# ConvGLU stage: block sums taken from the high and low parts of the stream, and one load list, five blocks ahead, for the down projection

## The chip, the core and the metric

The kernel runs on one core of one Trainium2 chip. Its engines are TensorE (PE; PEld is its weight load), VectorE (DVE), ScalarE (ACT), GpSimd (POOL) and SyncE (SP). SP issues most DMAs; POOL and ACT have queues of their own. The metric is the device time of one execution in microseconds (us); the time of a kernel is the median over runs. All arithmetic is in float32.

## What is computed

One layer of a hybrid backbone over 1024 latent tokens of width 1024 (and 256 context tokens): a mixer, an output projection with a gated residual, then a gated feed-forward network with a 3x3 depthwise convolution on its gate branch, and a last norm. The change lies in the feed-forward part, which is, with x the stream after the mixer (D_FF is 2816):

```python
h = modulate(rmsnorm(x, norm2_g), shift2, scale2)
g = h @ ffn_w_gate                       # 1024 x 2816
u = h @ ffn_w_up
g = dwconv2d_grid(g, conv_w, conv_b)     # 3x3 over a 16 x 64 grid
x = x + gate2 * ((silu(g) * u) @ ffn_w_down)
out = rmsnorm(x, final_norm_g)
```

## The kernel before

**High and low parts.** A float32 product is made of three TensorE products: each operand r is cast to a rounded h (`nc.scalar.copy`, on ACT), and l = r - h is taken on DVE (`tt`) or POOL (`ptt`); then hh, hl and lh are added in PSUM. `split` (L1444) does this for a weight block of 128x512 and gives tiles `wh` and `wl`. `raw` (L1434) loads a block into one of 20 buffers named `rw` by a DMA of the SP queue.

**Norm of the feed-forward's input.** `norm2(t)`, L1313 to L1333, runs for each of 8 tiles of 128 tokens: sum of squares on ACT (into the tile `u`, two buffers), `ss` to a power on POOL, scale on DVE, shift on POOL or DVE, 8 transposes on PE into two PSUM banks `bk`, then for each bank the cast into `mxh` (ACT, L1327) and the low part into `mxl` (DVE). It also copies each bank back over `u` (ACT, L1331) and stores that to DRAM (`ub_d`, SP, L1332), and it stores the stream for the last residual (`x1_d`, SP, L1333; the trace and the lists call it `x_d`).

**First gate and up blocks.** The first two gate columns are plain products of `mxh`, `mxl` (`fmm`, L1302). Their results `im` go through `conv`: for each of two images one ACT instruction and eight taps, `fac<-im,v,fac` at L107 on DVE. The first two up products follow (`up0`), also at L1302.

**Eleven pairs by seven products.** The other 10 pairs of gate columns and 10 of up columns (with `NP` = 11 pairs in all) are made by a seven-product scheme (`group7`, L1519, `bmm` at L1464): seven products of 12 matmuls in place of eight. It needs sums of weight blocks (`rw<-rw,rw`, POOL) and four sums of stream blocks T1 to T4. The four blocks B11, B12, B21, B22 of the transposed stream come back from `ub_d` for these, 16 loads of 256 KB; DVE subtracts, ACT casts into `tq`, and DVE or POOL takes the low parts. T4 overwrites a block that the first products still read, so its cast (L1629) comes after `up0`.

**Sums for the down projection.** While pair j runs, `asums(j)` stores seven blocks of silu(g)*u and their sums to `sa_d`, and `wsums(j)` loads four blocks of `ffn_w_down` and stores their four sums to `sw_d`. `wsums(10)` comes after the last product of the last group.

**Down projection.** Seven products P1, P4, P2, P6, P7, P5, P3 of 11 blocks each, 12 matmuls to a block, at L1692 (`mul`, `product`). A block needs two loads of 256 KB, one from `sa_d` and one from `ffn_w_down` or `sw_d`, both split with the low part on DVE. Each block's loads are written where it is used. P3 has 8 blocks that are split early and stay on the chip (`ahead`, L1757). The stream for the residual, `x1r`, 8 loads of 512 KB (L1713), and the row `gfrow` (L1728) are loaded by SP, written after P1.

**What sets the order.** A scheduler decides at build time in which order each engine runs its instructions, from the order in which they are written and from the buffers that they wait for. Each engine and each DMA queue then takes its list strictly in order.

Of the kernel before, what the change touches and what calls it, by code (L numbers as in the profile page):

```python
# [13 lines left out]
ALU = mybir.AluOpType  # L14
# [59 lines left out]
def hybrid_layer(ctx: ExitStack, tc: tile.TileContext, x, c, cx, c_ctx, w_ada, b_ada, norm1_g, w_in,  # L74
# [69 lines left out]
    ub_d = [T(drp, [NLC, P, 512], f"ub_d{i}") for i in range(2)]  # L144
# [1160 lines left out]
    with pool("op") as op:  # L1305
# [9 lines left out]
        def norm2(t):  # L1315
# [4 lines left out]
            pbs = []  # L1320
            for i in range(2):
# [93 lines left out]
    ASUM = "DDPP"  # L1415
    NR = NTL // GW
# [102 lines left out]
    def group7(w, fa, fb):  # L1519
        st = {}  # L1520

        def prep(n):
            if n == 0:
                st["a11"], st["a21"], st["a22"], st["a12"] = (
                    raw(wcols(w, i, f)) for (i, f) in ((0, fa), (0, fb), (1, fb), (1, fa)))
# [65 lines left out]

    im0 = first_im
# [3 lines left out]
    upw0 = [[raw(wcols(w_up, i, f)) for i in range(2)] for f in FORD[:2]]  # L1596


    late_t4 = []
    for u in range(4):  # L1600
        b11, b12, b21, b22 = (raw(ub_d[i][u + 4 * h]) for i in range(2) for h in range(2))
        t1, t2 = raw(), raw()
        tt(t1, b12, b11, ALU.subtract)
        tt(t2, b22, t1, ALU.subtract)
        tt(b12, b22, b12, ALU.subtract)
        tt(b21, t2, b21, ALU.subtract)
        for n_, t, on_pool in (("T2", t2, u % 2), ("T3", b12, 1), ("T1", t1, u % 2)):
            h, l = (m[:, u, :, :].rearrange("p k t -> p (k t)") for m in BLK[n_])
            nc.scalar.copy(h, t)
            (ptt if on_pool else tt)(l, t, h.bitcast(F32), ALU.subtract)  # L1610
        late_t4.append(b21)
        if u == 1:
            ups_ = [split(r, False) for r in upw0[0]]

    up0 = []
    for b in range(2):
        if b:
            ups_ = [split(r) for r in upw0[1]]
# [8 lines left out]
    for u in range(4):  # L1627
        h, l = (m[:, u, :, :].rearrange("p k t -> p (k t)") for m in BLK["T4"])
        nc.scalar.copy(h, late_t4[u])  # L1629
        ptt(l, late_t4[u], h.bitcast(F32), ALU.subtract)  # L1630
# [9 lines left out]
    preps, ready = {}, {}  # L1640
    AHEAD = 4

    def prepare(i):
        k, j, n = prods[i]
        if n == 0:
            preps[k, j] = group7(w_gate if k == "g" else w_up, FORD[2 * j], FORD[2 * j + 1])
        ready[i] = preps[k, j](n)
# [4 lines left out]
    for i, (k, j, n) in enumerate(prods):  # L1652
# [25 lines left out]
    STA = dict(P1=0, P2=1, P4=2, P3=3, P5=4, P6=5, P7=6)  # L1678
    MOV = dict(P5=0, P6=1, P7=2, P4=3)
    WD = dict(P1=(0, 0), P2=(1, 0), P3=(1, 1))  # L1680

    def sources(p, j):
        if p in MOV:
            return sa_d[STA[p]][j], sw_d[MOV[p]][j]
        k, d = WD[p]
        return sa_d[STA[p]][j], w_down[(j + NP * k) * P:(j + NP * k + 1) * P, 512 * d:512 * d + 512]
# [7 lines left out]
    def product(p, acc, js, first, last, between=None):  # L1694
        for j in js:
            ops = [split(raw(src), False) for src in sources(p, j)]
            for t in range(4):
                mul(acc[t], t, ops, first and j == js[0], last and j == js[-1])
            if between is not None:
                between(j)  # L1700
# [11 lines left out]
    for t in range(NLC):  # L1712
        nc.sync.dma_start(x1[t], x1_d[t])  # L1713
# [14 lines left out]
    nc.sync.dma_start(gf, final_norm_g.partition_broadcast(P))  # L1728
# [24 lines left out]

    HEAD = NP - NLC
    rest = []

    def ahead(*at):  # L1757
        def f(j):
            if j not in at:
                return  # L1760
# [82 lines left out]
```

## Time and profile before

| | |
|---|---|
| runs of the kernel before, us | 1575.12, 1579.88, 1582.5; median 1579.88 |
| the profiled execution, us | 1586.62, of which its span 1584.9 |
| granted TensorE clock over the span | 0.954 |
| busy: PE, DVE, POOL, ACT | 1414.9 (89%), 1159.8 (73%), 793.6 (50%), 745.9 (47%) |
| mixer | to about 790 us |
| output projection, `norm2`, first gate and up blocks | 790 to 909.7 us |
| pairs by seven products | 921.96 to 1336.5 us |
| down projection | 1359.43 to about 1577 us |

The times of a row of the trace are start and length in us. Matmuls are pipelined, so a row of 0.39 us stands for one that takes 0.23 us of PE in a row of them. A bracket at the end of a row gives how long the engine had been idle and which instruction or DMA ended that.

### The profile page before, as it was taken

What the parts mean: (1) busy time and instruction counts of PE and PEld (TensorE: products, weight loads), DVE (VectorE), ACT (ScalarE), POOL (GpSimd) and SP (SyncE); (2) the same over time, 40 slices, a digit from 0 to 9 for tenths busy, and PEclk for the clock granted to TensorE, in tenths of its full rate; (3) what the DMA queues carried; (4) which work ended last, traced back from release to release, by engine and by line L of the source; (5) the groups of instructions that cost most, each with busy time, mean ns of one, the idle gap of its engine ahead of it and who ended that gap; (6) DMA issues with size and microseconds to landing.
All of it is one profiled execution on the core that took longest, in us unless ns stands there. A gap on an engine that the chain in (4) does not pass through costs nothing. (4 is left out here: it accounts for less than half of the span.)

```text
span 1584.9 us, 24483 instructions
## 1 busy us (share of the span) xinstructions
PE 1414.9 (89%) x8104; PEld 1170.3 (74%) x8104; DVE 1159.8 (73%) x1861; ACT 745.9 (47%) x1671; POOL 793.6 (50%) x778
## 2 busy tenths in 40 slices
PE   6899888899998899998985958999999997699997
PEld 2477777787888789997764746877777775588786
DVE  5877698887545757457975679989988997357686
ACT  6566655636666746444254243333333331355453
POOL 3554499782216874201381287678888885000001
PEclk8999999999999999999996979999999999799999
DMA  7344777654669774436953243444444443966732
GB/s 265 122 144 136 233 223 211 162 147 115 181 193 305 224 236 149 152 96 229 336 191 139 96 144 107 146 159 154 152 147 160 153 153 132 399 216 212 216 115 106
DMA packets 273917, 283.54 MB, mean 179 GB/s; under 512 B 52448, under 2 KB 195421, under 8 KB 273791
## 3 DMA queue, kind: packets, MB, share of 16 engines
q1 hardware_dynamic: 266991, 261.41, 52.0%
q0 software_dynamic: 5456, 17.82, 3.1%
q10 hardware_dynamic: 1344, 2.75, 0.5%
q8 instruction: 64, 1.05, 0.3%
q14 instruction: 62, 0.51, 0.1%
HBM read 200.26 MB, written 81.65 MB: 178 GB/s over the span
## 5 line engine op out<-in xcount | busy, mean ns | idle before, releaser
L1444 ACT CAST wh<-rw 128x512 fp32r<-128x512 f32 x282 | 164.7, 620 | 311.2 <-POOL rw L98 107.8
L98 POOL TENSOR_TENSOR wl<-rw,wh 128x512 fp32r<-128x512 f32 x142 | 197.5, 1408 | 88.6 <-ACT wh L1444 85.2
L107 DVE SCALAR_TENSOR_TENSOR fac<-im,v,fac 128x945 f32<-128x945 f32 (+2 forms) x176 | 210.2, 1211 | 33.2 <-ACT fac L92 31.8
L1464 PE MATMUL pb<-mxh,wh 128*128 128x512 f32 x320 | 128.0, 400 | 29.2 <-ACT wh L1444 12.3
L1464 PE MATMUL pb<-tq,wh 128*128 128x512 f32 x480 | 147.3, 391 | 4.2 <-ACT wh L1444 4.2
L95 DVE TENSOR_TENSOR wl<-rw,wh 128x512 fp32r<-128x512 f32 x140 | 92.6, 701 | 61.5 <-ACT wh L1444 61.5
L456 PE MATMUL bk<-hh,wh 128*128 128x512 f32 x320 | 130.0, 407 | 1.6 <-ACT up L506 0.9
L456 PE MATMUL bk<-hh,wl 128*128 128x512 f32 x320 | 130.2, 407 | 0.0
L456 PE MATMUL bk<-hl,wh 128*128 128x512 f32 x320 | 129.0, 403 | 0.0
L1464 PE MATMUL pb<-mxl,wh 128*128 128x512 f32 x320 | 126.8, 396 | 0.3 <-POOL mxl L98 0.3
L1464 PE MATMUL pb<-mxh,wl 128*128 128x512 f32 x320 | 126.5, 395 | 0.0
L1747 POOL TENSOR_TENSOR ss<-ss,mhalf 128x1 f32<-128x1 f32 x8 | 7.3, 918 | 231.8 <-DVE ss L95 231.7
L98 POOL TENSOR_TENSOR rw<-rw,rw 128x512 f32<-128x512 f32 x80 | 110.1, 1387 | 10.5 <-DMA rw<-in_ffn_w_up_dram 5.5
L1464 PEld LDWEIGHTS pb<-tq,wh 128*128 128x128 f32 x480 | 90.4, 189 | 24.1 <-ACT wh L1444 5.4
L1464 PEld LDWEIGHTS pb<-mxh,wh 128*128 128x128 f32 x320 | 61.3, 192 | 46.0 <-issue 16.4
L1464 PE MATMUL pb<-tq,wl 128*128 128x512 f32 x240 | 92.0, 390 | 2.0 <-POOL wl L98 2.0
L95 DVE TENSOR_TENSOR rw<-rw,rw 128x512 f32<-128x512 f32 x60 | 68.7, 1166 | 8.2 <-DMA sa_d<-rw 5.6
L456 PEld LDWEIGHTS bk<-hh,wh 128*128 128x128 f32 x320 | 62.0, 194 | 14.4 <-ACT up L506 1.1
L456 PEld LDWEIGHTS bk<-hh,wl 128*128 128x128 f32 x320 | 61.9, 193 | 13.2 <-issue 0.9
L1692 PE MATMUL im<-wh,wh 128*128 128x512 f32 x144 | 51.0, 395 | 23.0 <-ACT wh L1444 23.0
L1464 PEld LDWEIGHTS pb<-mxl,wh 128*128 128x128 f32 x320 | 61.5, 192 | 13.2 <-POOL mxl L98 0.7
L1464 PEld LDWEIGHTS pb<-mxh,wl 128*128 128x128 f32 x320 | 61.4, 192 | 13.1
(410 smaller groups left out, 4148.3 us busy)
## 6 DMA issues: line engine op xcount, KB each, us to landing
rw<-in_ffn_w_down_dram SPq DMA_DIRECT2D x77, 256.0 KB
rw<-sa_d SPq DMA_DIRECT2D x77, 256.0 KB
kv<-kv_d SPq DMA_DIRECT2D x80, 192.0 KB
yq<-yq_d SPq DMA_DIRECT2D x64, 192.0 KB
awa<-in_w_ada_dram SPq DMA_DIRECT2D x24, 512.0 KB
rw<-in_ffn_w_up_dram SPq DMA_DIRECT2D x44, 256.0 KB
sa_d<-fac SPq DMA_DIRECT2D x44, 256.0 KB
sw_d<-rw SPq DMA_DIRECT2D x44, 256.0 KB
```

The source lines that it names most:

```text
L95: nc.vector.tensor_tensor(o, a, b, op=op)
L98: nc.gpsimd.tensor_tensor(o, a, b, op=op)
L107: nc.vector.scalar_tensor_tensor(o, a, s, b, op0=op0, op1=op1)
L456: paced(nc.tensor.matmul(pb[:, :bn], w[i][:, kk, :], hview(h, k, b0, bn), start=(n == 0), stop=(n == 3 * KT - 1)))
L1444: nc.scalar.copy(h, r)
L1464: nc.tensor.matmul(pv, w[:, q], m[:, :, k, :], start=(n == 0), stop=(n == 11))
L1692: nc.tensor.matmul(pb, a[:, tk], w, start=start and n == 0, stop=stop and n == 2)
L1747: nc.gpsimd.tensor_tensor(rs, rs, mhalf[:, 0:1], op=ALU.pow)
```

## The change

1. `norm2` neither copies the banks back into `u` nor stores them; `ub_d` and its 16 loads are gone. The store of `x1_d` is issued by POOL, no longer by SP.
2. The blocks for T1 to T4 are made on DVE as h + l of `mxh` and `mxl`, 16 more instructions, and this is written ahead of the first convolution. T4's sums wait in `sm` tiles. A table says which engine takes a low part: DVE still takes four of them and POOL twelve. The low parts of the first up weights move from DVE to POOL.
3. `group7` loads its four blocks when it is made, and the first group is made before `up0`.
4. `wsums(10)` moves to the fourth product of the last group. All 77 blocks of the down projection stand in one list, and a block's loads are issued five blocks ahead; those of the first five are written in the last group's first five products.
5. `x1r` and `gfrow` are loaded by POOL's queue.

```diff
@@ norm2
-            pbs = []
...
-                pbs.append(pb)
-            for i in range(2):
-                nc.scalar.copy(u[:, 512 * i:512 * i + 512], pbs[i])
-                nc.sync.dma_start(ub_d[i][t], u[:, 512 * i:512 * i + 512])
-            nc.sync.dma_start(x1_d[t], x1[t])
+            nc.gpsimd.dma_start(x1_d[t], x1[t])
@@ group7
+        st["a11"], st["a21"], st["a22"], st["a12"] = (
+            raw(wcols(w, i, f)) for (i, f) in ((0, fa), (0, fb), (1, fb), (1, fa)))
@@ sums of stream blocks
+    TPOOL = ((0, 1, 0, 1), (1, 1, 1, 1), (1, 1, 1, 1), (0, 1, 0, 1))
+    for u in range(4):
+        r = {}
+        for (n_, t0, k0) in (("11", 0, 0), ("12", 4, 0), ("22", 4, 4), ("21", 0, 4)):
+            r[n_] = raw()
+            h, l = (m[:, t0 + u, k0:k0 + 4, :].rearrange("p k t -> p (k t)").bitcast(F32) for m in mxs)
+            tt(r[n_], h, l, ALU.add)
+        t1, t2 = raw(), raw()
+        t4.append(sm())
+        tt(t1, r["12"], r["11"], ALU.subtract)
...
+        tparts("T2", u, t2, TPOOL[0][u])
+        tparts("T3", u, r["12"], TPOOL[1][u])
+        tparts("T1", u, t1, TPOOL[2][u])
+        if u == 0:
+            ups_ = [split(w) for w in upw0[0]]
     im0 = first_im
     for b in range(2):
         acs[0, b] = fac(FORD[b])
         conv(FORD[b], im0[b], acs[0, b])
-        b11, b12, b21, b22 = (raw(ub_d[i][u + 4 * h]) for i in range(2) for h in range(2))
...
-            ups_ = [split(r, False) for r in upw0[0]]
+    groups = {("g", 1): group7(w_gate, FORD[2], FORD[3])}
@@ the loop over the products of the pairs
-        if k == "g" and n == 3:
-            wsums(j - 1)
+        if n == 3 and (k == "g" or j == NP - 2):
+            wsums(j - 1 if k == "g" else NP - 1)
+        if (k, j) == ("u", NP - 1) and n < 5:
+            load(n)
...
-            if j == NP - 1:
-                wsums(j)
@@ down projection
+    def load(i):
+        if i < len(blocks):
+            loaded[blocks[i]] = [raw(src) for src in sources(*blocks[i])]
+    LD = 5
-    def product(p, acc, js, first, last, between=None):
+    def product(p, acc, js, first, last):
         for j in js:
-            ops = [split(raw(src), False) for src in sources(p, j)]
+            i = blocks.index((p, j))
+            load(i + LD)
+            ops = [split(r, False) for r in loaded.pop((p, j))]
...
-        nc.sync.dma_start(x1[t], x1_d[t])
+        nc.gpsimd.dma_start(x1[t], x1_d[t])
-    nc.sync.dma_start(gf, final_norm_g.partition_broadcast(P))
+    nc.gpsimd.dma_start(gf, final_norm_g.partition_broadcast(P))
```

The order on ACT in the last three token tiles of `norm2`, before (L92 into `u` is the sum of squares, L1327 the cast, L1331 the copy back):

```order
L92 ACTIVATE u_9587,ss_141<-x_6_8736 128x1024
L1327 CAST mxh<-bk_9548 128x512
L1331 COPY u_9535<-bk_9541 128x512
L1331 COPY u_9535<-bk_9548 128x512
L92 ACTIVATE u_9639,ss_141<-x_7_8737 128x1024
L1327 CAST mxh<-bk_9593 128x512
L1327 CAST mxh<-bk_9600 128x512
L1331 COPY u_9587<-bk_9593 128x512
L1331 COPY u_9587<-bk_9600 128x512
```

and with the change, in the same place:

```order
L92 ACTIVATE u_9561,ss_139<-x_6_8734 128x1024
L1325 CAST mxh<-bk_9519 128x512
L1325 CAST mxh<-bk_9526 128x512
L92 ACTIVATE u_9609,ss_139<-x_7_8735 128x1024
L1325 CAST mxh<-bk_9567 128x512
L1325 CAST mxh<-bk_9574 128x512
```

The copies between a cast and the next sum of squares are gone; the sum of squares of tile 7 stands ahead of the casts of tile 6, as before.

On DVE at the first convolution, before (`fac<-im` is a tap, `wl` the low part of an up weight, `rw<-rw,rw` a sum for T1 to T4):

```order
L95 TENSOR_TENSOR mxl<-bk_9652,mxh 128x512
L107 SCALAR_TENSOR_TENSOR fac_9820<-im_9675,v_122,fac_9820 128x15x63
L107 SCALAR_TENSOR_TENSOR fac_9822<-im_9676,v_122,fac_9822 128x15x63
L107 SCALAR_TENSOR_TENSOR fac_9820<-im_9675,v_122,fac_9820 128x960
L95 TENSOR_TENSOR wl_9873<-rw_9824,wh_9872 128x512
L95 TENSOR_TENSOR wl_9877<-rw_9826,wh_9876 128x512
L107 SCALAR_TENSOR_TENSOR fac_9822<-im_9676,v_122,fac_9822 128x960
L107 SCALAR_TENSOR_TENSOR fac_9820<-im_9675,v_122,fac_9820 128x15x63
L95 TENSOR_TENSOR rw_9840<-rw_9834,rw_9832 128x512
```

and with the change (`rw<-mxh,mxl` is a new sum h + l):

```order
L95 TENSOR_TENSOR mxl<-bk_9622,mxh 128x512
L107 SCALAR_TENSOR_TENSOR fac_9886<-im_9641,v_120,fac_9886 128x15x63
L95 TENSOR_TENSOR rw_9794<-mxh,mxl 128x512
L95 TENSOR_TENSOR rw_9796<-mxh,mxl 128x512
L95 TENSOR_TENSOR rw_9798<-mxh,mxl 128x512
L95 TENSOR_TENSOR rw_9800<-mxh,mxl 128x512
L107 SCALAR_TENSOR_TENSOR fac_9888<-im_9642,v_120,fac_9888 128x15x63
L107 SCALAR_TENSOR_TENSOR fac_9886<-im_9641,v_120,fac_9886 128x960
L95 TENSOR_TENSOR rw_9802<-rw_9796,rw_9794 128x512
L107 SCALAR_TENSOR_TENSOR fac_9888<-im_9642,v_120,fac_9888 128x960
```

The new sums are written ahead of the first convolution, but the list has none of them ahead of its first tap. Four stand between the first tap of the one image and the first of the other, the other twelve in groups of four among the later taps.

On SP between the last group and the down projection, before (`sa_d<-` and `sw_d<-` are stores of the pairs' sums, `rw<-sa_d_102` is the first load of a block of P1; the last store to `sa_d` stands just ahead of these):

```order
L1434 DMA rw_13584<-in_ffn_w_down_dram 128x512
L1434 DMA rw_13586<-in_ffn_w_down_dram 128x512
L1713 DMA x1r_13873<-x_d 128x1024
L1713 DMA x1r_13874<-x_d 128x1024
L1713 DMA x1r_13875<-x_d 128x1024
L1713 DMA x1r_13876<-x_d 128x1024
L1503 DMA sw_d_112<-rw_13588 128x512
L1713 DMA x1r_13877<-x_d 128x1024
L1713 DMA x1r_13878<-x_d 128x1024
L1434 DMA rw_13604<-sa_d_102 128x512
L1503 DMA sw_d_113<-rw_13589 128x512
```

and with the change, first at the loads of the first five blocks, ten in all (`rw_13421`, `rw_13422` and `fac_12887` belong to pair 9):

```order
L1509 DMA sa_d_107<-rw_13421 128x512
L1509 DMA sa_d_108<-fac_12887 128x512
L1429 DMA rw_13455<-sa_d_102 128x512
L1509 DMA sa_d_105<-rw_13422 128x512
L1429 DMA rw_13457<-in_ffn_w_down_dram 128x512
L1429 DMA rw_13478<-sa_d_102 128x512
```

then behind them, at the loads of the sixth (`fac_13239`, `rw_13575` and `rw_13576` belong to pair 10):

```order
L1509 DMA sa_d_102<-fac_13239 128x512
L1509 DMA sa_d_107<-rw_13575 128x512
L1429 DMA rw_13594<-sa_d_102 128x512
L1509 DMA sa_d_108<-fac_13239 128x512
L1429 DMA rw_13596<-in_ffn_w_down_dram 128x512
L1509 DMA sa_d_105<-rw_13576 128x512
```

The loads of the first five blocks stand behind the stores of pair 9 and ahead of those of pair 10; the loads of the sixth block (`rw_13594`) stand behind those of pair 10. The loads of `x1r` are off this list; on POOL they stand right behind the last sum of pair 10, `rw_13576`.

## Rows read from the trace of the kernel before

**Rows 1.** Busy time of each engine in four stretches of 50 us: stretch, its length, busy us (instructions) of PE, PEld, DVE, ACT and POOL, granted PE clock, share of the DMA engines busy, GB/s moved.

```profile
900.00:950.00 50.00, 31.96 (x129) 24.98 (x128) 38.30 (x39) 20.98 (x33) 40.78 (x28) 0.83 0.37 115
950.00:1000.00 50.00, 44.02 (x182) 35.55 (x181) 47.74 (x51) 15.96 (x23) 36.05 (x28) 0.93 0.29 101
...
1350.00:1400.00 50.00, 40.57 (x171) 33.43 (x172) 21.50 (x33) 22.49 (x40) 0.00 (x0) 0.87 0.95 353
1400.00:1450.00 50.00, 49.64 (x220) 40.76 (x219) 26.87 (x42) 25.68 (x47) 0.00 (x0) 1.00 0.70 219
```

**Rows 2.** What PE waited for from 800 to 1000 us: tile and line that waited, what it waited for, us in total, times, longest.

```profile
PE pb L1464 <- ACT wh L1444: 15.8, 2, 12.3
PE bk L1325 <- DVE u L95: 15.6, 4, 4.6
```

**Rows 3.** The same view from 1300 to 1585 us.

```profile
PE im L1692 <- ACT wh L1444: 23.0, 1, 23.0
```

**Rows 4.** The time line of PE in `norm2`: the transposes of the first and the last of five token tiles (those between start at 841.58, 847.93 and 854.49), and the first gate product.

```profile
834.99 1.97 PE L1325 MATMUL bk<-ident,u 128*128 128x128 f32 x8 [5.05 <-POOL u L98]
...
860.06 1.94 PE L1325 MATMUL bk<-ident,u 128*128 128x128 f32 x8 [3.63 <-DVE u L95]
861.65 0.78 PE L1302 MATMUL im<-mxh,gh 128*128 128x512 f32 x1
```

**Rows 5.** The time line of ACT in `norm2`: the sum of squares of one token tile, with the store that it waited for.

```profile
842.51 1.06 ACT L92 ACTIVATE u<-x 128x1024 f32<-128x1024 f32 x1 [2.25 <-DMA ub_d<-u]
```

**Rows 6.** The time line of DVE in `norm2`: its work for one token tile.

```profile
843.69 0.15 DVE L104 TENSOR_SCALAR ss<-ss 128x1 f32<-128x1 f32 x1 [2.26 <-ACT u L92]
844.17 0.69 DVE L95 TENSOR_TENSOR mxl<-bk,mxh 128x512 fp32r<-128x512 f32 x1 [0.32 <-ACT mxh L1327]
844.78 1.28 DVE L107 SCALAR_TENSOR_TENSOR u<-x,ss,sc2row 128x1024 f32<-128x1024 f32 x1
845.97 0.68 DVE L95 TENSOR_TENSOR mxl<-bk,mxh 128x512 fp32r<-128x512 f32 x1
846.57 1.22 DVE L95 TENSOR_TENSOR u<-u,sh2row 128x1024 f32<-128x1024 f32 x1
```

**Rows 7.** The time line of DVE from the first tap to the first group's sums.

```profile
881.08 1.20 DVE L107 SCALAR_TENSOR_TENSOR fac<-im,v,fac 128x945 f32<-128x945 f32 x1 [17.73 <-ACT fac L92]
886.52 2.33 DVE L107 SCALAR_TENSOR_TENSOR fac<-im,v,fac 128x945 f32<-128x945 f32 x2 [4.23 <-ACT fac L92]
888.76 2.89 DVE L95 TENSOR_TENSOR wl<-rw,wh 128x512 fp32r<-128x512 f32 x2
...
896.69 1.28 DVE L95 TENSOR_TENSOR rw<-rw,rw 128x512 f32<-128x512 f32 x2
...
915.79 1.19 DVE L107 SCALAR_TENSOR_TENSOR fac<-im,v,fac 128x945 f32<-128x945 f32 x1
...
923.76 1.75 DVE L95 TENSOR_TENSOR rw<-rw,rw 128x512 f32<-128x512 f32 x1
...
937.69 0.69 DVE L95 TENSOR_TENSOR sm<-pb,sm 128x512 f32<-128x512 f32 x1 [8.82 <-PE pb L1464]
```

**Rows 8.** ACT and POOL ahead of the first group: the second silu, the first weight cast of the group, and POOL's two last low parts before PE's last wait there.

```profile
919.80 1.09 ACT L92 ACTIVATE fac<-fac 128x1024 f32<-128x1024 f32 x1
...
921.26 0.65 ACT L1444 CAST wh<-rw 128x512 fp32r<-128x512 f32 x1
...
933.69 2.51 POOL L98 TENSOR_TENSOR wl<-rw,wh 128x512 fp32r<-128x512 f32 x2
```

**Rows 9.** PE at the first group: the waits that are left in the time line.

```profile
921.96 0.79 PE L1464 MATMUL pb<-mxh,wh 128*128 128x512 f32 x1 [12.26 <-ACT wh L1444]
...
935.01 0.50 PE L1464 MATMUL pb<-tq,wl 128*128 128x512 f32 x1 [1.96 <-POOL wl L98]
```

**Rows 10.** DVE's sums of 128x512 over the whole span, from the profile page's costliest groups: busy us, mean ns of one.

```profile
L95 DVE TENSOR_TENSOR rw<-rw,rw 128x512 f32<-128x512 f32 x60 | 68.7, 1166 | 8.2 <-DMA sa_d<-rw 5.6
```

**Rows 11.** SP's queue at the entry to the down projection (its rows are the issue, not the transfer).

```profile
1326.99 1.69 SPq L1514 DMA_DIRECT2D sa_d<-rw  x2
...
1341.08 0.32 SPq L1514 DMA_DIRECT2D sa_d<-rw  x1
...
1343.06 1.93 SPq L1713 DMA_DIRECT2D x1r<-x_d  x4
...
1346.99 0.44 SPq L1434 DMA_DIRECT2D rw<-sa_d  x1
```

**Rows 12.** ACT's first cast of the down projection, and PE from the last matmul of the pairs on.

```profile
1356.83 0.62 ACT L1444 CAST wh<-rw 128x512 fp32r<-128x512 f32 x1 [30.02 <-DMA rw<-sa_d]
...
1336.07 0.39 PE L1464 MATMUL pb<-mxh,wl 128*128 128x512 f32 x1
1359.43 1.22 PE L1692 MATMUL im<-wh,wh 128*128 128x512 f32 x2 [22.97 <-ACT wh L1444]
...
1363.01 0.52 PE L1692 MATMUL im<-wh,wl 128*128 128x512 f32 x1
1363.37 0.40 PE L1692 MATMUL im<-wh,wh 128*128 128x512 f32 x1
```

**Rows 13.** DMAs issued by POOL: what the issue cost POOL (busy us, mean ns), and, from the list of issues on the page, a transfer of 512 KB with its median us from issue to landing.

```profile
L562 POOL DMA_DIRECT2D kv_d<-rs x4 | 3.6, 912 | 0.0
...
kv_d<-rs POOLq DMA_DIRECT2D x4, 512.0 KB, 4.6
```

More of the change, by code (lines that the diff above doesn't have):

```diff
@@ L1627, in hybrid_layer, with sources @@
     for u in range(4):
-        h, l = (m[:, u, :, :].rearrange("p k t -> p (k t)") for m in BLK["T4"])
-        nc.scalar.copy(h, late_t4[u])
-        ptt(l, late_t4[u], h.bitcast(F32), ALU.subtract)
+        tparts("T4", u, t4[u], TPOOL[3][u])
+    STA = dict(P1=0, P2=1, P4=2, P3=3, P5=4, P6=5, P7=6)
+    MOV = dict(P5=0, P6=1, P7=2, P4=3)
+    WD = dict(P1=(0, 0), P2=(1, 0), P3=(1, 1))
+    def sources(p, j):
+        if p in MOV:
+            return sa_d[STA[p]][j], sw_d[MOV[p]][j]
+        k, d = WD[p]
+        return sa_d[STA[p]][j], w_down[(j + NP * k) * P:(j + NP * k + 1) * P, 512 * d:512 * d + 512]
+    HEAD = NP - NLC
+    DORD = ("P1", "P4", "P2", "P6", "P7", "P5", "P3")
+    ATS = dict(P4=(9,), P2=(5,), P6=(2, 8), P7=(3, 8), P5=(4, 8))
+    blocks = []
+    n_ = HEAD
+    for p in DORD:
+        for j in range(HEAD if p == "P3" else NP):
+            blocks.append((p, j))
+            if j in ATS.get(p, ()):
+                blocks.append(("P3", n_))
+                n_ += 1
+    assert n_ == NP
+    loaded = {}
+    def load(i):
+        if i < len(blocks):
+            loaded[blocks[i]] = [raw(src) for src in sources(*blocks[i])]
+    LD = 5
     seq7 = []
@@ L1692, in mul, with resident @@
             nc.tensor.matmul(pb, a[:, tk], w, start=start and n == 0, stop=stop and n == 2)
-    def product(p, acc, js, first, last, between=None):
+    rest = []
+    def product(p, acc, js, first, last):
         for j in js:
-            ops = [split(raw(src), False) for src in sources(p, j)]
+            i = blocks.index((p, j))
+            load(i + LD)
+            ops = [split(r, False) for r in loaded.pop((p, j))]
             for t in range(4):
                 mul(acc[t], t, ops, first and j == js[0], last and j == js[-1])
-            if between is not None:
-                between(j)
+            if j in ATS.get(p, ()):
+                load(i + 1 + LD)
+                resident(*blocks[i + 1])
+    def resident(p, j):
+        u = len(rest)
+        ops = []
+        for i, r in enumerate(loaded.pop((p, j))):
+            th, tl = (m[:, u, 4 * i:4 * i + 4, :].rearrange("p k c -> p (k c)") for m in mxs)
+            nc.scalar.copy(th, r)
+            tt(tl, r, th.bitcast(F32), ALU.subtract)
+            ops.append((th, tl))
+        rest.append(ops)
     imA = [image() for _ in range(2)]
@@ L1781, in hybrid_layer @@
         put(t, LOH, m)
-    product("P6", accB, allj, True, True, ahead(2, 8))
+    product("P6", accB, allj, True, True)
     for t in range(4):
@@ L1786, in hybrid_layer @@
         tt(s2[:, t, :], accB[t], s1[:, t, :], ALU.add)
-    product("P7", accA, allj, True, True, ahead(3, 8))
+    product("P7", accA, allj, True, True)
     for t in range(4):
@@ L1794, in hybrid_layer @@
         half1(4 + t, LOH)
-    product("P5", accB, allj, True, True, ahead(4, 8))
+    product("P5", accB, allj, True, True)
     for t in range(4):
```

63 lines of the change are left out of this document (16 added, 47 removed).

## The prediction

> **What bounds the kernel now.** I first read the busy time by stretches [rows 1]. PE is near its limit in the down projection (220 matmuls in 50 us, one in 0.227 us, at the full clock of 2.4 GHz), and loses time in two places: 900 to 950 us, with 31.96 us busy, and 1350 to 1400 us, with 40.57 us busy while the DMA engines are busy for 0.95 of the time. So only work on the way into and out of these two places counts. Then the waits of PE by their cause. Ahead of the pairs PE waits 15.8 us for weight casts on ACT and 15.6 us for the shifted stream `u` that DVE makes for `norm2` [rows 2]; at the entry to the down projection it waits once, 23.0 us, for a cast [rows 3]. Last I followed each wait back in the time lines, as told below.
>
> **The front: norm2.** The transposes of five token tiles start between 834.99 and 860.06 us, 6.27 us apart in the mean, each behind a wait for `u` [rows 4]. A round is a circle: the sum of squares goes into `u`, which still holds a copied bank, so that it waits for the store to `ub_d`, 2.25 us in the row [rows 5]; then come power, scale, shift, transposes, casts and the copies. The change takes the copies and stores out (16 instructions on ACT, 16 stores on SP), and by ACT's new order the sum of squares of a tile runs while the tile before is in work. What is left in a round is DVE's own work, 0.15 + 0.69 + 1.28 + 0.68 + 1.22 = 4.02 us [rows 6]. Four rounds then save 4 x (6.27 - 4.02) = 9.0 us. The store of the stream, now on POOL, costs POOL some 0.91 us to issue, by the row of a 512 KB store [rows 13]; POOL's power for a tile stands in the same list. If the two never overlapped DVE's work, four rounds would lose 4 x 0.91 = 3.6 us of the nine; I take them as hidden, since a round leaves POOL 4 us. The 16 loads from `ub_d` go from SP's queue; what DVE reads instead is on the chip already.
>
> **DVE in the first convolution.** The change adds 16 sums h + l of 128x512. The nearest rows, sums between two tiles, are 0.64 us each while POOL is quiet (two in 1.28) and 1.75 us where POOL works beside it [rows 7]; over the span such a sum takes 1.166 us in the mean [rows 10]. The order puts four of the new sums between the first taps of the two images, where DVE was idle for 4.23 us [rows 7]: these are hidden. The 17.73 us before the first tap stay idle, as no sum stands ahead of it. Twelve sums lie among the later taps, 12 x 0.64 = 7.7 us; the two low parts of the first up weights leave DVE, 2.89 us [rows 7]. So the last tap, which started at 915.79 us, moves by -9.0 + 7.7 - 2.9 = -4.2 us. Behind it stand, on ACT, the two silus and then the first weight cast of the group, at 921.26 [rows 8], for which PE had waited 12.26 us [rows 9]: PE starts the pairs 4.2 us earlier. The last wait of this place, 1.96 us at 935.01, is for a low part on POOL [rows 8, 9]. POOL takes two low parts more (some 2.5 us, as the pair in [rows 8]) but starts nine earlier, so its chain gains 6 to 7 us. Between the two I take **-6 us** for the front. The bounds: all nine and a little of the first round, -10; with each of the twelve sums at 1.166 us, 14.0 us, the last tap comes at -9.0 + 14.0 - 2.9 = +2.
>
> It is a gain for the whole span only if it lives through the pairs. DVE is busy for 47.74 of 50 us from 950 to 1000 [rows 1], but it waited 8.82 us for PE just ahead of that [rows 7], so it has no backlog to keep, and PE, which sets the pace later, hands on what it gained.
>
> The Trainium skill ("SBUF — State Buffer", section "SBUF: two separate sides") speaks against this part: a DVE instruction with two SBUF inputs and a POOL instruction exclude each other for the whole instruction. The rows agree, 0.64 us against 1.75 us; by that rule all twelve sums cost more, and the front would come to nothing, as in the first rival.
>
> **The entry to the down projection.** PE's last matmul of the pairs starts at 1336.07 and the next at 1359.43 [rows 12]. ACT's cast ahead of it waited 30.02 us for a load from `sa_d` [rows 12], which SP issued only at 1346.99, behind the stores of pair 10, the loads for `wsums(10)` and six loads of `x1r` [rows 11]; it landed 9.84 us later among all that traffic. In the changed list this load stands behind the stores of pair 9, which SP issued from 1326.99 to 1328.7 [rows 11]. So it is issued at about 1328; if it takes the 9.84 us of the crowd it lands at 1338, if it takes the 4.6 us of a transfer of 512 KB on POOL's queue [rows 13], at 1333. Cast and low part add 0.62 and about 0.7 us. PE is free at 1336.3, so it waits 0 to 3 us in place of 22.97; I take 1. The long wait also cost clock: nine matmuls from 1359.43 to 1363.37 took 3.94 us, in rows of 0.63 us (1.2 GHz), where nine at 0.227 take 2.04 us [rows 1, 12]; this 1.9 us goes too. The loads for `wsums(10)` stand ahead of pair 9's stores, and its four sums and the first low parts fit DVE's waits in the last group.
>
> Late next is the sixth block. Its loads stand behind the stores of pair 10, the last of which was issued at 1341.08 [rows 11]; five blocks of 12 x 0.227 = 2.72 us keep PE to about 1351. At the same time POOL issues the loads of `x1r` and `gfrow`, nine times 512 KB, 4.7 MB. A block needs 0.52 MB in 2.72 us, 193 GB/s, and the engines moved 353 GB/s in this stretch [rows 1], so 160 are left for POOL's queue, which needs some 29 us; nothing needs `x1r` before the third product. I charge 1 us. Sum: 22.97 - 1 + 1.9 - 1 = 22.9, taken as **-23 us**; bounds -25 (no wait at all) and -15 (see the second rival).
>
> The Trainium skill ("DMA: Bandwidth & Descriptors", "Queues, rings and completion order") has each DMA engine alternate between the queues that have work. By it P1 would get half of 353, 176 GB/s, for 27 us and fall behind by 0.45 MB, less than a block; no run here shows the two queues against each other yet.
>
> **Sum.** -6 - 23 = -29 us. The profiled execution took 1586.62 us (span 1584.9), 0.4% above the median of 1579.88; I carry the difference over: 1557.6 for such an execution, and **1551 us** for the median.
>
> **Rivals.** (1) DVE eats the front: its new sums meet POOL's low parts, front +2 instead of -6, DVE busy without a break from the first tap on. For it: 1.75 us in [rows 7] and the mean of 1.166. Against: POOL waits for the same sums and starts late. 1579.9 + 2 - 23 = 1559 us. Chance 0.22.
> (2) The two queues share badly: rows of `x1r` are twice as long as those of a block, and if POOL's queue gets two thirds of 353, 235 GB/s, P1 has 118 against 193 for 20 us and lacks 1.5 MB, 2.9 blocks, 7.8 us: entry -15, sum -21, 1559 us. For it: the share of 0.95. Against: a lead of five blocks. Chance 0.13.
> (3) Slower: POOL's queue goes first. Nine transfers of 4.6 us each [rows 13] would hold the engines from 1342 to 1383, and the sixth block, wanted at 1351, could be cast at about 1386. PE then waits 35 us: -6 - 23 + 35 = +6, 1586 us. It decides from a wait of over 29 us at the sixth block. Against it: before, loads of both kinds in one queue ran at 353 GB/s together. Chance 0.06.
> (4) The change doesn't do what it says: the early loads sit behind pair 9's last sums on DVE, which slip, and half of the wait stays: -6 - 12, 1562 us. Chance 0.04.
>
> **The numbers.** The forecast has a chance of 0.55. The low end is -10 - 25 = -35, 1545, less the 4.8 us by which the fastest run of before lies under its median: 1540. The high end takes in rivals 1, 2 and 4, the first two also together (+2 - 15 = -13, 1567): 1568. Outside lie rival 3 and the far ends of the rest. A measurement of this kernel tells about 0.5%, 7.9 us, from no change. All cases but the third are faster by more than that, 0.94, less 0.02 for several mishaps together: 0.92. The third lies at the bound, 1586 against 1587.8, so its 0.06 and those 0.02 go half to each side: 0.04 within it, 0.04 slower.
>
> **What would show it.** Right: transposes of `norm2` about 4 us apart; the first group from about 918 us; the four first sums of DVE between the two first taps; the first load of P1 issued ahead of the last product, PE's wait at the entry under 3 us and its matmuls there at 0.39 us; no wait at the sixth block. Wrong: a DVE sum of over 1.2 us in the convolution, a wait of PE of several us between 1350 and 1385, or transposes still 6 us apart.

## The result and the profile after

| | before | after |
|---|---|---|
| runs, us | 1575.12, 1579.88, 1582.12, 1582.5 | 1560.25, 1560.26, 1561.85, 1562.9 |
| median, us | 1581.00 | 1561.05 |
| ratio to before, 95% interval | | 0.9882 [0.9854, 0.991] |
| profiled execution, span, us | 1586.62, 1584.9 | 1562.9, 1561.1 |
| granted TensorE clock over the span | 0.954 | 0.961 |

The change makes the kernel about 20 us faster. Forecast were 29 us and 1551; the time lies inside the range, 10 us above the forecast. The two profiled executions show where (the point of reference is the last matmul of the output projection; only the norm of the first token tiles runs beside it):

| stage of PE, us | before | after | difference |
|---|---|---|---|
| to the last matmul of the output projection | 828.68 | 826.66 | -2.0 (within the spread: 820.7 to 828.3 in the other twelve executions) |
| from there to the third group from the end | 449.8 | 443.5 | -6.3 |
| last three groups, to the last matmul of the pairs | 57.6 | 64.6 | **+7.0** |
| from there to the first matmul of the down projection | 23.4 | 0.2 | **-23.1** |
| down projection, first to last matmul | 217.3 | 217.9 | +0.6 |

These add up to the 23.8 us by which the spans differ. The idle time at the entry is gone whole, and the front gave what was forecast; but seven microseconds came back in the last three groups, where the prediction had put nothing, and the down projection is no faster although its first nine matmuls now run at full clock.

Waits of PE from 800 to 1000 us (first two rows) and from 1300 to 1561 us, after, with the columns of [rows 2, 3]:

```profile
PE pb L1459 <- ACT wh L1439: 19.6, 2, 17.8
PE bk L689 <- POOL aac L98: 7.8, 1, 7.8
...
PE bk L1323 <- DVE u L95: 5.1, 2, 2.7
...
PE pb L1459 <- DVE fac L95: 4.5, 1, 4.5
PE im L1717 <- ACT wh L1439: 2.2, 3, 1.0
```

The waits for `u` fell from 15.6 to 5.1 us (2.6 more are now put down to `ss`), and 23.0 us for one cast became 2.2 for three. Three rows have grown: the wait for weight casts ahead of the first group, a new one for POOL at the last row of the modulation (`aac`), and a wait for `fac` at the last group that was 0.32 us before.

The time line of PE, after, at the places of [rows 4, 9, 12] and at the last group (start, length, idle time and its releaser):

```profile
827.77 1.09 PE L1323 MATMUL bk<-ident,u 128*128 128x128 f32 x8
836.65 2.07 PE L689 MATMUL bk<-aac,ones 128*128 128x512 f32 x2 [7.79 <-POOL aac L98]
838.51 1.92 PE L1323 MATMUL bk<-ident,u 128*128 128x128 f32 x8
843.05 1.07 PE L1323 MATMUL bk<-ident,u 128*128 128x128 f32 x8 [2.62 <-DVE ss L104]
846.79 1.94 PE L1323 MATMUL bk<-ident,u 128*128 128x128 f32 x8 [2.67 <-DVE u L95]
851.13 1.94 PE L1323 MATMUL bk<-ident,u 128*128 128x128 f32 x8 [2.40 <-DVE u L95]
852.73 0.78 PE L1301 MATMUL im<-mxh,gh 128*128 128x512 f32 x1
...
919.03 0.80 PE L1459 MATMUL pb<-mxh,wh 128*128 128x512 f32 x1 [17.80 <-ACT wh L1439]
...
931.21 0.50 PE L1459 MATMUL pb<-tq,wl 128*128 128x512 f32 x1 [0.72 <-POOL wl L98]
...
1313.27 0.76 PE L1459 MATMUL pb<-mxh,wh 128*128 128x512 f32 x1 [4.55 <-DVE fac L95]
...
1334.80 0.39 PE L1459 MATMUL pb<-mxh,wl 128*128 128x512 f32 x1
1335.03 0.62 PE L1717 MATMUL im<-wh,wh 128*128 128x512 f32 x2
...
1356.00 0.73 PE L1717 MATMUL im<-wh,wh 128*128 128x512 f32 x2 [0.99 <-ACT wh L1439]
...
1360.07 0.73 PE L1717 MATMUL im<-wh,wh 128*128 128x512 f32 x2 [0.79 <-ACT wh L1439]
...
1363.78 0.73 PE L1717 MATMUL im<-wh,wh 128*128 128x512 f32 x2 [0.43 <-ACT wh L1439]
```

The last four transposes of `norm2` are 3.7 to 4.5 us apart in place of 6.27; between the one ahead of them and theirs lie 10.7 us, with the wait of 7.79 us for POOL. The pairs end at 1334.80 and the next product starts 0.23 us later, with no bracket. Behind the 4.55 us at 1313.27 twelve matmuls are 0.43 us apart, at a granted clock of 0.50 (1.2 GHz; stretch, length, busy us of PE, clock, DMA share, GB/s):

```profile
1313.30:1318.00 4.70, 4.70 (x11) 0.50 0.43 167
```

The time line of DVE, after, at the first convolution [rows 7] and ahead of the last group:

```profile
871.46 1.20 DVE L107 SCALAR_TENSOR_TENSOR fac<-im,v,fac 128x945 f32<-128x945 f32 x1 [17.04 <-ACT fac L92]
872.58 2.49 DVE L95 TENSOR_TENSOR rw<-mxh,mxl 128x512 f32<-128x512 f32 x4
876.89 2.33 DVE L107 SCALAR_TENSOR_TENSOR fac<-im,v,fac 128x945 f32<-128x945 f32 x2 [1.83 <-ACT fac L92]
...
885.10 3.58 DVE L95 TENSOR_TENSOR rw<-mxh,mxl 128x512 f32<-128x512 f32 x4
...
896.25 2.48 DVE L95 TENSOR_TENSOR rw<-mxh,mxl 128x512 f32<-128x512 f32 x4
...
906.33 3.55 DVE L95 TENSOR_TENSOR rw<-mxh,mxl 128x512 f32<-128x512 f32 x4
...
913.84 1.19 DVE L107 SCALAR_TENSOR_TENSOR fac<-im,v,fac 128x945 f32<-128x945 f32 x1
...
1303.70 1.22 DVE L95 TENSOR_TENSOR rw<-rw,rw 128x512 f32<-128x512 f32 x1
...
1308.34 2.48 DVE L95 TENSOR_TENSOR rw<-rw,rw 128x512 f32<-128x512 f32 x2
...
1313.05 0.68 DVE L95 TENSOR_TENSOR pb<-pb,sm 128x512 f32<-128x512 f32 x1
...
1314.82 0.68 DVE L95 TENSOR_TENSOR rw<-rw,rw 128x512 f32<-128x512 f32 x1
```

The first tap starts 9.6 us earlier than before, the last one only 1.95 us earlier, and those 2.0 us are the ones gained upstream, by chance. The rows at 1303.70 and 1308.34 are three sums of `wsums(10)`; they stand ahead of DVE's instruction at 1313.05, and PE's wait ends right behind that.

The issue queues, after, at the entry [rows 11, 12]: SP's, then ACT's first cast of the down projection, then POOL's.

```profile
1325.54 0.42 SPq L1429 DMA_DIRECT2D rw<-sa_d  x1
...
1340.03 0.45 SPq L1429 DMA_DIRECT2D rw<-sa_d  x1
...
1328.39 0.62 ACT L1439 CAST wh<-rw 128x512 fp32r<-128x512 f32 x1 [2.19 <-DMA rw<-sa_d]
...
1342.77 4.25 POOL L1753 DMA_DIRECT2D x1r<-x_d  x8 [0.30 <-POOL rw L98]
```

The first load of P1 is issued 9.3 us ahead of the last matmul of the pairs and is cast 2.85 us later; before, it was issued at 1346.99. The sixth block's load goes out at 1340.03, and the eight loads of `x1r` follow it 2.7 us later on the other queue.

### The profile page after: what moved, and what is told of

The parts are those of the page before. It is cut to its first block, busy times and chain, and to the rows that moved or that the text cites. A ratio compares the mean times of both kernels' runs of the same rounds, so it can differ in the third digit from the quotient of the medians.

```text
span 1561.1 us, 24442 instructions
## 1 busy us (share of the span) xinstructions
PE 1417.2 (91%) x8104; PEld 1172.1 (75%) x8104; DVE 1174.8 (75%) x1875; ACT 738.5 (47%) x1655; POOL 809.8 (52%) x797
## 5 line engine op out<-in xcount | busy, mean ns | idle before, releaser
L455 PEld LDWEIGHTS bk<-hl,wh 128*128 128x128 f32 x320 | 61.7, 193 | 12.1 <-issue 0.2
```

Source lines behind the costliest of these rows:

```text
L455: paced(nc.tensor.matmul(pb[:, :bn], w[i][:, kk, :], hview(h, k, b0, bn), start=(n == 0), stop=(n == 3 * KT - 1)))
```

## The experiments

The theory after the result: the entry gives its full 25 us, but (a) `wsums(10)` in the last group but one delays DVE's combinations, which PE awaits, and (b) `x1r` on POOL's queue holds up the loads of P1 more than the 1 us charged. The rivals were that the earlier front brings the wait at the last group, and that the front lost its part to the new sums. Where two of the experiments are said to differ by less than their intervals, it is the traces that separate them.

**Each half alone.** The front (`norm2` and the block sums) with the old entry:

```diff
-        if n == 3 and (k == "g" or j == NP - 2):
-            wsums(j - 1 if k == "g" else NP - 1)
-        if (k, j) == ("u", NP - 1) and n < 5:
-            load(n)
+        if k == "g" and n == 3:
+            wsums(j - 1)
... the down projection as before
```

> The changed kernel with the entry to the down projection put back: each block's loads where it is used, wsums(10) after the last product of the pairs, x1r and gfrow loaded by SP. In the changed kernel the first gate product came 8.9 us earlier, PE's last wait ahead of the pairs 3.8 us earlier, and the pairs were 8.3 us ahead at 1270 us. Theory (the front's gain lives through the pairs, and the 7 us that were lost again around 1313 us belong to wsums(10)): the pairs end 6 to 8 us earlier than before, no wait of PE for DVE over 1.5 us in the last two groups, the idle time of 23 us at the entry stays; about 7 us under the kernel before, 1572 to 1575. Rival (DVE sets the pace at the end of the pairs, and whatever the front gains is taken back there): a wait of 4 to 5 us at the last group here too, the pairs end 1 to 2 us earlier, 1578 to 1580.

Measured: 1574.86, ratio 0.9968 [0.9944, 0.9992], which is 5.1 us (1.3 to 8.8). PE's wait at the last group is 0.83 us, that at the entry 23.33 us.

The entry alone, with `norm2`, the round trip through `ub_d` and the sums as before:

```diff
... norm2, the loads of b11 to b21 from ub_d and the place of group7 as before;
... kept: wsums(NP - 1) in the last group but one, the list, x1r on POOL
```

> The changed kernel with norm2 and the sums for T1 to T4 put back (copies, stores to and loads from ub_d); the list of loads, wsums(10) moved ahead and x1r on POOL's queue stay. Theory: the entry gives 23 us of idle time and 1.9 of clock, less 2 to 3 us in the first blocks, less about 7 us that wsums(10) costs ahead of the last group, whatever the front does: 15 to 18 us under the kernel before, 1563 to 1566, with a wait of PE for DVE of 4 to 5 us at the start of the last group. Rival (the wait at the last group comes of the earlier front): no such wait, 21 to 23 us under before, 1558 to 1560.

Measured: 1565.08, 0.9914 [0.9881, 0.9947]: 13.6 us by the ratio and 14.1 by the medians, of the 23 forecast. PE waits 5.42 us at the last group, although the front is the old one. So the earlier front does not bring this wait; the entry's own edits do. By the ratios the halves add up to 18.6 us, against 18.7 of both together.

**`wsums(10)` at its old place,** behind the last product, with the list kept:

```diff
-        if n == 3 and (k == "g" or j == NP - 2):
-            wsums(j - 1 if k == "g" else NP - 1)
+        if k == "g" and n == 3:
+            wsums(j - 1)
@@ behind the last asums
+            if j == NP - 1:
+                wsums(j)
```

> The changed kernel with wsums(10) alone put back to where it was, after the last product of the pairs; the blocks' loads stay early. Its sums are first needed eleven blocks, some 30 us, later. Theory (its four sums, 4.4 us on DVE just ahead of the last group, are what PE waited 4.55 us for at 1313 us, and the idle time cost another 2.6 us at the lower clock): the wait at the last group falls under 1.5 us, the pairs end about 7 us earlier, and DVE takes the sums beside the first blocks without PE waiting over 1 us more: about 7 us under the changed kernel, 1553 to 1556. Rival (the wait has another cause, or DVE lacks the 4.4 us at the entry instead): 1560 to 1562.

Measured: 1567.44, 0.9938 [0.9913, 0.9962], 6 us slower than the change by the medians and 9 by the ratios. The wait at the last group is gone (0.99 us), but two others come in its place. PE's waits, then SP's queue, then DVE, in this kernel:

```profile
1354.72 1.22 PE L1719 MATMUL im<-wh,wh 128*128 128x512 f32 x2 [7.96 <-ACT wh L1439]
1362.91 0.73 PE L1719 MATMUL im<-wh,wh 128*128 128x512 f32 x2 [2.71 <-ACT wh L1439]
...
1343.00 0.33 SPq L1498 DMA_DIRECT2D sw_d<-rw  x1
1343.37 0.97 SPq L1429 DMA_DIRECT2D rw<-sa_d  x1
...
1349.07 0.92 SPq L1498 DMA_DIRECT2D sw_d<-rw  x2
1350.09 0.38 SPq L1429 DMA_DIRECT2D rw<-sa_d  x1
...
1348.35 1.90 DVE L95 TENSOR_TENSOR rw<-rw,rw 128x512 f32<-128x512 f32 x3 [4.79 <-DMA rw<-in_ffn_w_down_dram]
```

DVE's last three sums wait 4.79 us for their loads, the stores of these sums wait for DVE, and in SP's list the loads of the next blocks stand behind the stores. The theory's 1553 to 1556 was wrong: moving `wsums(10)` ahead of the entry is a part of the entry's gain. What is wrong with it is only the engine or the group it was moved to.

**`wsums(10)` on POOL, or one group later.**

```diff
     def wsums(j):
+        tt = ptt if j == NP - 1 else dve_tt
```

> The changed kernel with the four sums of wsums(10) on POOL in place of DVE, at the same place and with the same loads. Theory (DVE sets the pace there, and its 4.4 us for these sums were PE's wait of 4.55 us at the last group; two groups without them waited 0.8 and 1.0 us): the wait at the last group is under 1.5 us, the pairs end 4 to 7 us earlier against the last matmul of the output projection, nothing is lost at the entry; 1554 to 1558. Rival (POOL, which makes the last group's low parts at the same time, then holds PE up): a wait of PE for POOL of 2 to 5 us in the last group, 1559 to 1563.

```diff
-        if n == 3 and (k == "g" or j == NP - 2):
+        if n == 3 and (k == "g" or j == NP - 1):
```

> The changed kernel with wsums(10) at the fourth product of the last group in place of that of the group before it. DVE has idle time there, as no convolution is left. Theory (DVE's time is the cost, and it is free in the last group): the wait at the last group is under 1.5 us and the pairs end 4 to 7 us earlier; the four loads of 256 KB now stand between those of the third and the fourth block, 1 to 2 us for them; 1555 to 1558. Rival (as with the sums after the last product, the stores of the sums hold the blocks' loads behind them on SP's queue): PE waits 4 us or more between the fourth and the seventh block, 1560 to 1567.

Measured: 1557.74, 0.9855 [0.9836, 0.9874], and 1557.78, 0.9856 [0.9831, 0.9882]. PE's wait at the last group is 1.03 and 0.83 us. From PE's wait at the third group from the end to the pairs' end, the six profiled executions with these sums on DVE in the group behind it take 63.0 to 65.5 us, seven without 57.7 to 59.2, and the kernel before 57.6. The means differ by 5.9 us: 4.1 us of wait, and 1.9 us that the last group itself takes longer, by its first matmuls at 0.43 in place of 0.23 us. Of this 3 to 4 us return at the entry, as waits of up to 2.4 us in each, since the sums now stand nearer to the first splits: from the last matmul of the pairs to the last of the down projection these two take 221.2 and 222.1 us, and the five executions with `x1r` on POOL's queue and the sums in the group before 218.3 in the mean.

**`x1r` and `gfrow` on SP again,** in the same place of the program, so behind the loads of the 16th block:

```diff
-        nc.gpsimd.dma_start(x1[t], x1_d[t])
+        nc.sync.dma_start(x1[t], x1_d[t])
...
-    nc.gpsimd.dma_start(gf, final_norm_g.partition_broadcast(P))
+    nc.sync.dma_start(gf, final_norm_g.partition_broadcast(P))
```

> The changed kernel with x1r and gfrow loaded by SP again; in SP's list they now come behind the loads of the sixteenth block of the down projection. Theory (on POOL's queue the 4.7 MB run beside the first blocks' loads, and PE's three waits of 0.99, 0.79 and 0.43 us from 1356 to 1364 are the whole price): those three waits go, 1 to 3 us under the changed kernel or the same, as the same bytes now come a little later on the one queue; 1558 to 1561. Rival (the early start on POOL's queue is worth something, as in one queue the nine loads stand in front of later blocks): a wait of PE of 3 us or more between 1380 and 1410, 1562 to 1568.

Measured: 1556.17, 0.9846 [0.9823, 0.9868]. The busy time from 1350 to 1400 us, after and then in this kernel, with the columns of [rows 1]:

```profile
1350.00:1400.00 50.00, 47.79 (x204) 37.34 (x203) 24.87 (x38) 25.92 (x46) 0.53 (x1) 1.00 0.96 355
```

```profile
1350.00:1400.00 50.00, 50.00 (x222) 41.44 (x221) 26.95 (x42) 27.62 (x50) 0.00 (x0) 1.00 1.00 374
```

With all loads in one queue PE is never idle in this stretch, and the engines move more, 374 against 355 GB/s. The loads of `x1r` are also issued 15 us later there, 22.6 us after the first matmul of the down projection in place of 7.7. PE starts its 180th matmul of the down projection 41.59 us after the first, against 45.33 in the change and 43.87 to 46.39 in the four other executions with POOL's queue and the sums in the same group: `x1r` on a queue of its own costs 3.7 us in the change, and 2.3 to 4.8 in all. The charge was 1 us.

The trace of the change has what each queue moved from 1350 to 1360 us (packets, MB, share of the 16 engines; q0 is POOL's queue, q1 SP's):

```profile
q0 software_dynamic: 742, 2.70, 66.9%
q1 hardware_dynamic: 741, 1.35, 35.5%
```

SP's queue, which feeds P1, got 135 GB/s where P1 needs 193; POOL's got twice as much.

**The store of the stream on SP again.**

```diff
-            nc.gpsimd.dma_start(x1_d[t], x1[t])
+            nc.sync.dma_start(x1_d[t], x1[t])
```

> The changed kernel with the store of the stream in norm2 issued by SP again. In the changed kernel PE waited 7.79 us at 836.65 for POOL's sums of the last row of the modulation, in whose list eight stores of 0.6 us stand, and the transposes of the fifth token tile waited behind it. Theory (DVE paces the token tiles from there on, and POOL's eight stores are hidden but for the 1 to 2 us that they put ahead of that sum): the first gate product comes 0 to 2 us earlier against the last matmul of the output projection; the same within 2 us, 1558 to 1562. Rival (POOL's issue is on the path of norm2, at 0.6 us for each tile): 3 to 5 us earlier, 1555 to 1558.

Measured: 1556.92, 0.9848 [0.9822, 0.9874]. The first gate starts 25.12 us after the output projection in place of 26.07. Only this one microsecond is seen to come from the edit; the interval overlaps that of the change, and the rest of the difference of 4 us stays open.

**All 16 sums on POOL, ahead of the first convolution.** POOL is idle there in the change.

```diff
+    for u in range(4):
...
+            ptt(r[n_], h, l, ALU.add)
...
-            tt(r[n_], h, l, ALU.add)
```

> The changed kernel with the 16 sums h + l on POOL, all written ahead of the first subtraction for T1 to T4. POOL was idle for 29.5 us from 847.9 on, and 16 sums at 1.25 us are 20 us. Theory (the front is bounded by DVE, which spent 12.1 us on sums between its first and last tap and was idle for 17.0 us ahead of them): the last tap starts about 10 us earlier, PE starts the pairs 8 to 11 us earlier (908 to 911 in place of 919.0), 6 to 10 us under the changed kernel, 1551 to 1555. Rival (POOL's own chain of low parts and weight sums bounds the front as soon as DVE does not): PE's first product is earlier but its last wait, for POOL at 931.2, moves by 3 us at most: 1558 to 1561.

Measured: 1558.35, 0.9873 [0.9828, 0.9918], not to be told from the change: the theory failed, and the rival held. POOL's time line and PE's waits at the first group:

```profile
846.90 21.86 POOL L98 TENSOR_TENSOR rw<-mxh,mxl 128x512 f32<-128x512 f32 x16
...
922.16 5.83 POOL L98 TENSOR_TENSOR rw<-rw,rw 128x512 f32<-128x512 f32 x4
...
914.35 0.80 PE L1459 MATMUL pb<-mxh,wh 128*128 128x512 f32 x1 [12.35 <-ACT wh L1439]
...
926.24 3.30 PE L1459 MATMUL pb<-tq,wh 128*128 128x512 f32 x6 [4.91 <-ACT wh L1439]
```

DVE's taps end some 19 us earlier against the output projection, and the first group starts 3.9 us earlier. Yet a later product of the same group waits 4.91 us, for a cast of a weight sum that POOL makes behind its low parts; the group ends and the next starts 119.2 us after the output projection, as in the change. So DVE's twelve sums among the taps are not what the front lacks: the rest of the group's preparation is as late.

**The pieces together,** in one comparison with the change: the change again; `wsums(10)` in the last group with both stores and loads on SP; `wsums(10)` on POOL with the same; and the second of these with the first group's weights loaded and split ahead of the block sums.

```diff
+    groups = {("g", 1): group7(w_gate, FORD[2], FORD[3])}
+    early = groups["g", 1](0)
     t4 = []
```

> The changed kernel once more, on the same chip and against the same runs as the combinations below, since the runs of one kernel differ by some 5 us. 20 to 24 us under the kernel before, a ratio of 0.985 to 0.988; a wait of PE for DVE of 4 to 5 us at the last group; from the first to the last matmul of the down projection 217 to 219 us.

> The changed kernel with wsums(10) in the last group, and with x1r, gfrow and the store of the stream on SP's queue. If the price of wsums(10) ahead of the last group (5.4 us from the last but one group's start to the end of the pairs) and that of the loads on POOL's queue (4 us in the down projection) add up: no wait over 1.5 us at the last group, 214 to 216 us from the first to the last matmul of the down projection, 7 to 10 us under the changed kernel of the same call. Rival (the loads for the sums still hold the fourth block's loads on SP's queue, whoever loads x1r): waits of 4 us in all between the third and the seventh block, 3 to 5 us under the changed kernel.

> The changed kernel with the four sums of wsums(10) on POOL, and with x1r, gfrow and the store of the stream on SP's queue. Theory: the wait at the last group is about 1 us, the waits of 1.27 and 2.32 us for the first blocks' casts and low parts remain, since POOL's sums delay the last group's parts; the three waits about the seventh block go; 6 to 9 us under the changed kernel of the same call. Rival: the waits of the first blocks grow when SP also has x1r: under 4 us.

> The kernel with wsums(10) in the last group and the three transfers on SP's queue, and besides the first group's weights loaded and its first block split ahead of the sums for T1 to T4. In all runs so far PE's first product of the pairs waited 12 to 18 us for a cast that stands behind the two silus on ACT. Theory (the sums for T1 to T4 end the front, not this cast): PE starts the pairs right after the first up products, at about 75 us from the output projection's last matmul in place of 92, and then waits as long for the second product; the tenth group starts 0 to 3 us earlier, the same within 3 us as without. Rival (the cast is what the front waits for): 5 us or more earlier at the tenth group.

| kernel | median us | ratio to before |
|---|---|---|
| the change again | 1561.49 | 0.9884 [0.9853, 0.9915] |
| last group, SP | 1551.65 | 0.9831 [0.9798, 0.9864] |
| on POOL, SP | 1553.68 | 0.9830 [0.9801, 0.9860] |
| last group, SP, early weights | 1557.33 | 0.9848 [0.9820, 0.9877] |

By the ratios the first two combinations are the fastest kernels of the study, about 27 us under the kernel before and 8 under the change; between themselves they can't be told apart. The pieces add up to the 8 us: the 5.9 us of the last three groups, 4.3 of POOL's queue (218.3 us in the mean to the end of the down projection, 214.0 with `x1r` on SP) and 1 of the store, less the 3 to 4 that return at the entry. One pair of profiled executions shows less: with `wsums(10)` in the last group the last three groups take 57.9 us (65.5 in the change again) and the down projection 217.0 (219.4; 214 to 216 were expected), but the stage ahead of them is 4.3 us longer, which is within the spread told below. The waits of PE from 1300 to 1565 us in the one with `wsums(10)` in the last group:

```profile
PE im L1717 <- DVE wl L95: 1.6, 1, 1.6
...
PE pb L1459 <- DVE fac L95: 0.6, 1, 0.6
```

With the early weights the kernel is slower by 5.7 us in the medians and 2.7 in the ratios, whose intervals overlap; what its trace shows is that the first group starts 99.6 us after the output projection, where the thirteen other executions have 88.5 to 93.3. Neither the theory nor the rival had that. PE there, then DVE:

```profile
923.90 0.80 PE L1459 MATMUL pb<-mxh,wh 128*128 128x512 f32 x1 [24.59 <-ACT rw L1630]
...
944.28 0.79 PE L1459 MATMUL pb<-mxh,wh 128*128 128x512 f32 x1 [4.47 <-DVE sm L95]
...
882.38 5.78 DVE L95 TENSOR_TENSOR rw<-mxh,mxl 128x512 f32<-128x512 f32 x4
...
915.22 5.68 DVE L95 TENSOR_TENSOR rw<-mxh,mxl 128x512 f32<-128x512 f32 x4
```

POOL, busy with the weights' low parts from 875.00 us, now works beside DVE's sums: the sixteen take 17.5 us in place of 12.1, and two fours of them 1.4 us each. PE's first product waits 24.59 us for a copy on ACT whose list waits for DVE. The wait for "ACT wh" ahead of the first group was never a matter of the weights alone.

## Why the prediction was right and wrong

**norm2: right in its sum, not in its steps.** The gate comes 6.9 us earlier against the output projection (8.9 by the clock on the wall), of 9.0 forecast. Four rounds were to shrink to DVE's own 4.02 us; three did, to 4.5, 3.7 and 4.3, which gives 5.9 us. The first, from the transposes at 827.77 to those at 838.51, grew from 6.6 to 10.7 us, as PE's list has the matmul of the modulation's last row between them and waits 7.79 us for POOL there. The sum comes out by luck: the transposes at 827.77 themselves stand 1.1 us after the output projection, in place of 6.3, and the sum had not counted that. The store on POOL, taken as hidden with 3.6 us as the most, makes up about 1 us of the 7.79: with the store on SP the same matmul still waits 5.25 us, for ACT.

**DVE's sums: the sum was wrong, its outcome right.** Four sums were hidden, 0.62 us each, as said. The other twelve took 3.58 + 2.48 + 3.55 = 9.6 us, not 7.7, as two of them met a low part on POOL, and the last tap did not move against the output projection (87.18 after it, 87.11 before): 0 in place of -4.2. Part of the 9 us was wasted, as PE's start shows: 0.9 us earlier, not 4.2. The front still gained, because later waits fell: 1.8 us at the end of the first group and at its last wait for POOL, where the text had put 6 to 7; 2.4 at the start of the third group, 4.7 at that of the sixth. At the third group from the end it is 4.4 in the mean of eleven profiled executions with the new `norm2` against the two with the old one (the eleven spread over 8 us), and by the ratio of the front alone 5.1. Forecast were 6, from two numbers of which neither came true: that the sum is near is luck in part. That the first rival (DVE eats the front) fails is shown; which of the later preparations gave the gain back is not. DVE and POOL there, one instruction each:

```profile
886.30 1.77 DVE L95 TENSOR_TENSOR rw<-mxh,mxl 128x512 f32<-128x512 f32 x1
```

```profile
896.45 3.44 POOL L98 TENSOR_TENSOR tq<-rw,tq 128x512 fp32r<-128x512 f32 x1 [1.67 <-ACT tq L1594]
```

A sum that meets a low part begun on POOL takes 1.77 us, the three beside it 0.68 each; a low part begun while DVE has four sums in a row takes 3.44 us, in place of about 1.3. The Trainium skill ("SBUF — State Buffer", "SBUF: two separate sides") has the two exclude each other for a whole instruction, and the trace agrees. But it does not follow that all twelve sums cost more, as the prediction says: only two of the twelve met one.

**The entry: right, and better than said.** The wait went from 22.97 us to none, the upper bound, and the lower clock of the nine matmuls with it.

**`wsums(10)`: the step that failed.** "Its four sums and the first low parts fit DVE's waits in the last group": the sums stand in the last group but one, in the fourth product (`j == NP - 2`; item 4 of the change and this sentence name the wrong group), and DVE has no waits there. From 1289.5 to 1321 us it has no idle time, and PE waits for what comes later there. Had I asked of this group what I asked of the entry (what is the last instruction that PE awaits, and what now stands ahead of it on that engine), the 4.55 us would have been in the sum. It costs 5.9 us with its clock, 7.0 in the profiled execution of the change. In the last group, where I believed the sums to be, PE's wait is under 1 us, but they cost 3 to 4 us at the entry: they would not have been free there either.

**The two queues: the second rival's mechanism, and a charge too small.** The rival's share is seen: two thirds of the bytes went to POOL's queue from 1350 to 1360 us. The loads of P1 came too slowly, with waits of 0.99, 0.79 and 0.43 us at the eighth to tenth block and stretched matmuls between; by the fifteenth block 3.7 us are lost, between my charge of 1 and the rival's 7.8. It is less than the rival had, since both queues together moved some 405 GB/s, not 353. The Trainium skill ("DMA: Bandwidth & Descriptors", "Queues, rings and completion order") has an engine alternate between the queues packet by packet, and the trace agrees, with 742 packets of the one beside 741 of the other. The half share that the prediction made of it was wrong, as the packets differ in size: 3.6 KB in the mean on POOL's queue and 1.8 KB on SP's, whose rows are half as long.

**The sum again,** for the entry: -22.97 - 1.9 + 3.7 + 5.9 = -15.3 us, where the entry alone measured -13.6 to -14.1; with the front's -5.1 it is -20.4, and -18.7 by the ratio, -20 by the medians, was measured. Both errors of the entry were in what the edit pushes work into, not in what it removes. That the time still lies inside the range is luck in part: the upper end was set for the first rival, which fails, and for the second, which is half there, and the 5.9 us of `wsums(10)`, which no rival had, fell into that room.

## What to carry to other kernels

When work is moved out of a gap, price the place where it lands by the same questions as the gap: which instruction there ends a wait last, and is the engine idle at all. Look the place up in the order and its row in the trace, by time and not by the name of the stage. And a load that nobody waits for is not free on another queue when the engines are saturated: put it behind the urgent ones in their own queue, where its place is certain.

## What the runs showed of the hardware

- Loads of two queues together moved 355 GB/s and starved the urgent one: the queue with rows of 4 KB got 270 GB/s and the one with rows of 2 KB 135, packet for packet. The same loads behind the urgent ones in one queue moved 374 GB/s, and PE had no wait.
- A short wait of PE has a second price. In the pairs the matmul behind a wait of 1.51 us (at 1191.36, after) takes 0.47 us; behind waits of 2.70 (1032.40) and 4.55 us (1313.27) it takes 0.77 and 0.76, and the next six and eleven are 0.43 us apart, which cost 2.4 us in the last case (granted clock 0.50). That such waits are why executions of one kernel differ by several microseconds is not shown.
- A store in an issue queue that waits for its data held the loads behind it for up to 8 us of PE's time (`wsums(10)` at its old place).
- Sixteen sums of 128x512 take POOL 21.86 us: 1.25 each while DVE is idle, 2.2 for two beside DVE. The same sum on DVE takes 0.62 us with POOL quiet, and 1.77 where it meets an instruction of POOL.
